# Second mixer of a two-layer encoder: activation tables fetched ahead, attention weights loaded beside the latent projection's, GpSimd multiplying its own taps in two of four channel tiles

## The chip, the cores and the metric

The kernel runs on one core of one Trainium2 chip. The metric is device time in microseconds (us) for one execution of the whole program. The kernel before takes 1110.24 us in the median of three runs (1110.16 to 1111.68).

## The reference

Two sequences of 256 tokens with 1024 features go through two layers. Each layer is a mixer and a feed-forward block, each followed by a residual sum and a layer norm. Only the second layer's mixer (`odd_mixer`) is touched:

```
h = x @ w_in                                   # 1024 -> 256 + 128 + 32 + 512 + 512
c_q, c_kv, k_r, glu_a, glu_g = split(h)
c = latent_attention(c_q, c_kv, k_r, ...)      # rmsnorm, q and k,v projections, rope, 8 heads, softmax
d = glu_a * sigmoid(glu_g)
d = silu(layernorm(dwconv(d, conv_w, conv_b))) # 31 taps along the tokens, 512 channels
return concat([c, d]) @ w_out
```

The other blocks are a first mixer (neighbourhood attention and spatial gating) and two convolutional feed-forward blocks of 2816 features (`ffn`).

## The kernel before

Both sequences are held together as 512 columns, features on the 128 partitions. Every product is done in three passes on a high and a low part (`hi`, `lo`) of weights and activations. A weight tile is fetched by SyncE's queue, rounded to `hi` by ScalarE (line 107) and reduced to `lo` by VectorE (line 109).

`odd_mixer` is written in the order glu(0), cproj, chain, glu(1), glu(2), kvproj, qproj, attend(0), glu(3), attend(1) to attend(3), flush, the first half of the output projection, the convolution's taps, `conv_ln`, the rest of the output projection. A scheduler with a model of the engines (`schedule_with_timeline_sim`) then sorts each engine's queue; each engine runs its queue strictly in order, and waits on semaphores for the others.

- `glu(i)` makes one of four tiles of 128 channels of the convolution's input (`dpad`): two products on TensorE, a sigmoid on ScalarE, a product on VectorE. It starts VectorE's accumulator `cacc` (tap 0 and the bias, in PSUM) and the second accumulator `acc` (`acc2` in the code).
- The 31 taps of a tile: VectorE does taps 0 to 20 on `cacc` (line 691). For taps 22 to 30 ScalarE multiplies (line 695, `pr`, a ring of two buffers) and GpSimd adds to `acc` (line 696); tap 21 starts `acc`. VectorE joins both (line 697).
- `cproj` and `chain` make the latent parts: after RMS norms and transposes, ScalarE writes the high and VectorE the low part of `cT` (lines 604, 605). `kvproj` and `qproj` read `cT` and write keys, values and queries.
- `attention` does a pair of heads and one sequence at a time. One unit (a head, a sequence) is: scores `s` on TensorE, row maximum `nmx` on VectorE (line 482), exponential on ScalarE (line 485), reciprocal `ri` on VectorE (line 488), scaling `er` on ScalarE (line 491), transposes `pt` on TensorE, a copy `PTr` on ScalarE (line 500). Two units are followed by one product `pv`. There are 16 units.
- `conv_ln` is the layer norm over the 512 channels: transposes `ct` to token tiles (four, t = 0 to 3), statistics on VectorE, the inverse root on GpSimd (line 162), the normalised `cnm` on VectorE, transposes `cb` back, Silu on ScalarE, and the split into `mixT[4..7]`. The last `ct` also releases GpSimd's residual products of tiles t = 2, 3 (`affine`).
- `OutProj`: its first group (attention's part) is summed by `op` (half 0) and `dn` (half 1) matmuls, its second group (the convolution's part) on top of them. The norm that follows ends in transposes `lnT`, and the next block starts with `up` matmuls.

Of the kernel before, what the change touches and what calls it, by code (L numbers as in the profile page):

```python
# [1 line left out]

# [6 lines left out]
F32 = mybir.dt.float32  # L9
# [3 lines left out]
ALU = mybir.AluOpType  # L13
# [37 lines left out]
def tile_encoder(ctx: ExitStack, tc: tile.TileContext, I, O):  # L51
# [46 lines left out]
    def after_mm(ins, m):  # L98
        tc.add_manual_dep(ins.ins, m.ins.name,
                          mybir.DependencyInfo(mybir.DependencyClass.Sync, mybir.DependencyReason.DATA),  # L100
                          reason="paced")

    def wload(src, n, keep=False):
        raw = rawp.tile([P, 1024], F32, tag="raw", name=nm("raw"))
# [24 lines left out]
    def pc(name, i):  # L129
        o, _ = PCOL[name]  # L130
        return par[:, o + i:o + i + 1]
# [152 lines left out]
    class OutProj:  # L284
# [12 lines left out]
        def step(self, k, t, half, w):  # L297
            gemm_tok([self.ps[half][t]], self.mixT[k], t, w[k][0], w[k][1], [slice(0, 512)],
                     k == self.g[0][0], k == self.g[1][-1])

        def first(self, half, ts=range(NT)):
            if self.ps[half] is None:
                self.ps[half] = [None] * NT if half == 0 else dn_banks()
                self.w1 = self.load(half, self.g[0])
            for t in ts:
                if half == 0:
                    self.ps[0][t] = bank(pA, "op0")
            for k in self.g[0]:
                for t in ts:
                    self.step(k, t, half, self.w1)  # L310
# [10 lines left out]
    def dn_banks():  # L321
        return [bank(pB if t < 2 else pC, "dn1") for t in range(NT)]
# [144 lines left out]
        return sink.xT  # L467

    pend = []

    def attention(p, score, V, mix, post, er, PTr, on_act=False):
        for s in range(2):
            PT = [PTr.get(), PTr.get()]
            pss = [bank(pB, "s").rearrange("p (a k) -> p a k", a=2) for _ in range(2)]
            for qt in range(2):
                for h in range(2):
                    score(pss[h][:, qt, :], h, slice(s * S + qt * P, s * S + qt * P + P), slice(s * S, s * S + S))
            for h in range(2):
                e = er.get()
                sc = post(pss[h], h, e)  # L480
                nmx = small(2, "nmx")
                nc.vector.tensor_reduce(out=nmx, in_=sc, axis=AX.X, op=ALU.max, negate=True)
                rs = small(2, "rs")
                for qt in range(2):
                    nc.scalar.activation(out=e[:, qt, :], in_=sc[:, qt, :], func=AF.Exp,
                                         bias=nmx[:, qt:qt + 1], accum_out=rs[:, qt:qt + 1])
                ri = small(2, "ri")
                nc.vector.reciprocal(out=ri, in_=rs)
                for qt in range(2):
                    if on_act:  # L490
                        nc.scalar.activation(out=e[:, qt, :], in_=e[:, qt, :], func=AF.Copy, scale=ri[:, qt:qt + 1])
                    else:
                        nc.vector.tensor_scalar(out=e[:, qt, :], in0=e[:, qt, :], scalar1=ri[:, qt:qt + 1],
                                                scalar2=None, op0=ALU.mult)
                pt = bank(pC, "pt")
                for kc in range(2):
                    for qt in range(2):
                        nc.tensor.transpose(pt[:, (2 * kc + qt) * P:(2 * kc + qt + 1) * P],  # L498
                                            e[:, qt, kc * P:(kc + 1) * P], ident)
                nc.scalar.copy(out=PT[h], in_=pt.rearrange("p (k q) -> p k q", k=2))  # L500

            def pv_stage(s=s, PT=PT):
                pv = bank(pC, "pv")
                for kc in range(2):
                    for h in range(2):
                        mm(pv[h * 64:(h + 1) * 64, :S], V[s][:, kc, (2 * p + h) * 64:(2 * p + h + 1) * 64],
                           PT[h][:, kc, :], kc == 0, kc == 1)
                split(mix, pv[:, :S], slice(s * S, s * S + S))
            flush_pv()
            pend.append(pv_stage)  # L510
# [10 lines left out]
    def odd_mixer(xT):  # L521
# [3 lines left out]
        def glu(i, by_seq=False):  # L525
            pss = []
            for hi, lo in kept.pop(i, None) or glu_load(i):
                pss.append((bank(pA, "glu"), hi, lo))
            for seqs in ((0,), (1,)) if by_seq else ((0, 1),):
                for ps, hi, lo in pss:  # L530
                    gemm_feat(ps, hi, lo, xT, seqs)
            sg = tmp([P, 512], s="sig")
            nc.scalar.activation(out=sg, in_=pss[1][0], func=AF.Sigmoid)
            d = dpad[i]
            nc.vector.tensor_tensor(out=d[:, :, 15:15 + S], in0=pss[0][0].rearrange("p (s t) -> p s t", s=2),
                                    in1=sg.rearrange("p (s t) -> p s t", s=2), op=ALU.mult)
            accps[i] = bank(pA, "cacc")
            a, a2 = accps[i].rearrange("p (s t) -> p s t", s=2), acc2[i // 2][:, i % 2]
            nc.vector.tensor_scalar(out=a, in0=d[:, :, 0:S], scalar1=pc("cw", i * 32),
                                    scalar2=pc("cw", i * 32 + 31), op0=ALU.mult, op1=ALU.add)  # L540
            nc.scalar.activation(out=a2, in_=d[:, :, 31 - NPOOL:31 - NPOOL + S], func=AF.Copy,  # L541
                                 scale=pc("cw", i * 32 + 31 - NPOOL))
# [14 lines left out]
        def cproj():  # L557
            psc = dn_banks()
            wc = [wload(I["wc"][:, 2 * k2:2 * k2 + 2, :].rearrange("p k n -> p (k n)"), 832) for k2 in range(4)]
            for s in range(2):  # L560
                for k in range(KC):
                    o = (k % 2) * 416
                    for t in (2 * s, 2 * s + 1):
                        gemm_tok([psc[t]], xT[k], t, *wc[k // 2], [slice(o, o + 416)], k == 0, k == KC - 1)
            G["psc"] = psc

        def chain():
# [27 lines left out]
            for i in (2, 0, 1, 3):  # L595
                w = P if i < 3 else 32
                for t in range(NT):
                    nc.tensor.transpose(ct_ps[i][0:w, t * P:(t + 1) * P],
                                        craw[t // 2][:, t % 2, i * P:i * P + w], ident)
                if i == 3:  # L600
                    nc.scalar.copy(out=krT[64:96, :], in_=ct_ps[3][0:32, :])
                else:
                    g = pc("qg", i) if i < 2 else pc("kvg", 0)
                    nc.scalar.activation(out=cT[i][:, 0, :], in_=ct_ps[i], func=AF.Copy, scale=g)
                    nc.vector.scalar_tensor_tensor(out=cT[i][:, 1, :], in0=ct_ps[i], scalar=g,
                                                   in1=cT[i][:, 0, :].bitcast(F32), op0=ALU.mult, op1=ALU.subtract)

        def qproj():
            cT = G["cT"]
            ropeT = act([P, 2, S], s="ropeT")  # L610
            after_mm(nc.gpsimd.dma_start(out=ropeT, in_=I["ropeT"]), G["start"])
            wq = [wload(I["wuq"][:, k, :], 1024) for k in range(2)]
            qT = G["qT"] = [act([P, 2, T], s="qT") for _ in range(4)]

            def qfeat(pool, c):
# [24 lines left out]

        def kvproj():
            cT, krT = G["cT"], G["krT"]
            wkv = wload(I["wukv"], 1024)
            V = G["V"] = [act([P, 2, 512], s="V1") for _ in range(2)]
            for t in range(NT):
                ps = bank(pB, "v1")
# [23 lines left out]
                      G["V"], mixT[p], lambda ps, h, e: ps, er, PTr, True)  # L670

        mixT = [None] * 8
        glu(0, True)
        cproj()
        chain()
# [1 line left out]
        glu(2)  # L677
        kvproj()
        qproj()
        attend(0)  # L680
        glu(3)
        for p in range(1, 4):
            attend(p)
        sink = G["sink"]
        flush_pv()
        op = OutProj("wout1", mixT, [0, 1, 2, 3], [4, 5, 6, 7])
        op.first(0, (0, 1))
        for i in range(4):
            a, a2 = accps[i].rearrange("p (s t) -> p s t", s=2), acc2[i // 2][:, i % 2]
            for j in range(1, 31 - NPOOL):  # L690
                nc.vector.scalar_tensor_tensor(out=a, in0=dpad[i][:, :, j:j + S], scalar=pc("cw", i * 32 + j), in1=a,  # L691
                                               op0=ALU.mult, op1=ALU.add)
            for j in range(32 - NPOOL, 31):
                pr = pr_ring.get()
                nc.scalar.activation(out=pr, in_=dpad[i][:, :, j:j + S], func=AF.Copy, scale=pc("cw", i * 32 + j))  # L695
                nc.gpsimd.tensor_tensor(out=a2, in0=a2, in1=pr, op=ALU.add)  # L696
            nc.vector.tensor_tensor(out=a2, in0=a, in1=a2, op=ALU.add)

        def conv_ln():
# [3 lines left out]
            for t in range(NT):  # L703
# [8 lines left out]
                n = tmp([P, 512], s="cnm")  # L712
                normalize(n, ps, mu, rstd)
                ns.append(n)
            for c in range(4):
                ps = bank(pA, "cb")
                for t in range(NT):
# [173 lines left out]
```

## Time and profile before

| what | us |
|---|---|
| median of three runs | 1110.24 |
| the profiled execution, whole | 1111.65 |
| its span | 1109.9 |
| TensorE busy in it | 1086.7 (98%) |
| VectorE, ScalarE, GpSimd busy in it | 663.3, 490.9, 224.0 |
| granted TensorE clock, mean | 0.986 |
| second mixer, from the first convolution input to the first `up` | about 574 to 738 |

The profile is of one execution. TensorE is busy nearly throughout, so the table of stages matters more than the totals: what can be won or lost is the time in which TensorE idles, or runs at a lower granted clock, in the second mixer.

### The profile page before, as it was taken

Reading aid. Unit: us, or ns where it says so; the run is one execution under the profiler, and the core shown is the slowest. Engines: PE = TensorE matmul, PEld = TensorE weight load, DVE = VectorE, ACT = ScalarE, POOL = GpSimd, SP = SyncE. Lnnn points to the kernel's source line nnn. Section 1 sums busy time; section 2 is a strip of 40 time slices with the busy share of each in tenths; the row PEclk is TensorE's granted clock in tenths of the full one; section 3 lists DMA queues with packets and bytes.
Section 4 is the critical chain, followed back from the end, with each engine's and each line's share of the span. In section 5 each row is a group of like instructions: output and inputs, shape, how many; then the busy total and the mean of one; then the engine's idle time right before and its main releaser. Section 6 shows DMA issues by size and latency. Waiting matters only on the chain. (4 is left out here: it accounts for less than half of the span.)

```text
span 1109.9 us, 13646 instructions
## 1 busy us (share of the span) xinstructions
PE 1086.7 (98%) x5210; PEld 902.8 (81%) x5210; DVE 663.3 (60%) x982; ACT 490.9 (44%) x789; POOL 224.0 (20%) x222
## 2 busy tenths in 40 slices
PE   9999999999999999999998979999999999999996
PEld 7888778988888888888897847789888888888885
DVE  5388956766565566422469897367656556552227
ACT  5435644544444444321365699446444444431110
POOL 0581002200000000006454757031000000000173
PEclk9999999999999999999999969999999999999998
DMA  7833222533333323654232221144333333222501
GB/s 263 247 107 95 72 101 96 171 95 97 96 101 103 98 95 114 197 184 138 76 117 76 60 93 67 57 135 132 96 97 101 103 98 96 95 95 95 211 36 76
DMA packets 36194, 124.34 MB, mean 112 GB/s; under 512 B 4353, under 2 KB 5121, under 8 KB 36129
## 3 DMA queue, kind: packets, MB, share of 16 engines
q1 hardware_dynamic: 28224, 99.00, 29.0%
q0 software_dynamic: 6480, 22.66, 5.9%
q10 hardware_dynamic: 1424, 1.80, 0.6%
q8 instruction: 41, 0.67, 0.3%
q14 instruction: 25, 0.20, 0.1%
HBM read 114.01 MB, written 8.39 MB: 110 GB/s over the span
## 5 line engine op out<-in xcount | busy, mean ns | idle before, releaser
L96 PE MATMUL up<-xT,whi 128*128 128x512 f32 (+1 forms) x1536 | 440.0, 371 | 0.0
L109 DVE TENSOR_TENSOR wlo<-raw,whi 128x1024 fp32r<-128x1024 f32 (+1 forms) x174 | 234.8, 1351 | 287.8 <-ACT whi L107 286.1
L96 PEld LDWEIGHTS up<-xT,whi 128*128 128x128 f32 x1536 | 279.9, 188 | 49.7
L107 ACT CAST whi<-raw 128x1024 fp32r<-128x1024 f32 (+1 forms) x174 | 182.3, 1050 | 246.3 <-PE dn L96 131.1
L96 PE MATMUL up<-xT,wlo 128*128 128x512 f32 (+1 forms) x768 | 283.8, 372 | 0.0
L96 PE MATMUL dn<-whi,gT 128*128 128x512 f32 x704 | 217.5, 389 | 0.0
L96 PEld LDWEIGHTS up<-xT,wlo 128*128 128x128 f32 x768 | 144.2, 188 | 25.1
L96 PEld LDWEIGHTS dn<-whi,gT 128*128 128x128 f32 x704 | 132.0, 188 | 27.2
L96 PE MATMUL dn<-wlo,gT 128*128 128x512 f32 x352 | 136.9, 389 | 0.0
L182 POOL DMA_DIRECT2D xres<-xscr x12 | 6.4, 540 | 574.7 <-PE dn L96 574.7
L96 PEld LDWEIGHTS dn<-wlo,gT 128*128 128x128 f32 x352 | 66.1, 188 | 13.7
L113 ACT CAST gT<-cv 128x512 fp32r<-128x512 f32 x44 | 27.3, 620 | 111.8 <-DVE cv L752 111.8
L741 ACT ACTIVATE cv<-up,par 128x512 f32<-128x512 f32 x88 | 68.2, 775 | 0.0
L744 DVE SCALAR_TENSOR_TENSOR cv<-up,par,cv 128x510 f32<-128x510 f32 x88 | 65.8, 748 | 2.7
L742 DVE SCALAR_TENSOR_TENSOR cv<-up,par,cv 128x510 f32<-128x510 f32 x88 | 65.4, 743 | 0.0
L751 ACT ACTIVATE cv<-cv 128x512 f32<-128x512 f32 x44 | 27.8, 632 | 83.3 <-DVE cv L744 83.3
L691 DVE SCALAR_TENSOR_TENSOR cacc<-dpad,par,cacc 128x512 f32<-128x512 f32 x80 | 59.0, 751 | 1.3
L696 POOL TENSOR_TENSOR acc<-acc,pr 128x512 f32<-128x512 f32 x36 | 49.9, 1386 | 37.3 <-ACT pr L695 35.2
L114 DVE TENSOR_TENSOR gT<-cv,gT 128x512 fp32r<-128x512 f32 x44 | 30.4, 692 | 27.5 <-ACT gT L113 27.5
L96 PE MATMUL op<-whi,mixT 128*128 128x512 f32 x128 | 44.0, 401 | 0.0
L96 PE MATMUL dn<-whi,mixT 128*128 128x512 f32 x128 | 43.0, 394 | 0.0
L96 PE MATMUL glu<-xT,khi 128*128 128x512 f32 (+1 forms) x160 | 42.2, 348 | 0.0
(192 smaller groups left out, 1348.0 us busy)
## 6 DMA issues: line engine op xcount, KB each, us to landing
raw<-in_wup SPq DMA_DIRECT2D x88, 512.0 KB, 3.7
raw<-in_wdn SPq DMA_DIRECT2D x44, 512.0 KB, 3.5
raw<-in_wout SPq DMA_DIRECT2D x16, 512.0 KB, 3.7
xscr<-xres POOLq DMA_DIRECT2D x12, 512.0 KB, 4.3
xres<-xscr POOLq DMA_DIRECT2D x12, 512.0 KB, 4.9
raw<-in_wqk SPq DMA_DIRECT2D x8, 512.0 KB, 5.8
raw<-in_wglu SPq DMA_DIRECT2D x8, 512.0 KB, 4.1
raw<-in_wug SPq DMA_DIRECT2D x7, 512.0 KB, 3.5
```

What stands on the lines that cost most here:

```text
L96: last_mm[0] = nc.tensor.matmul(out=out, lhsT=lhsT, rhs=rhs, start=first, stop=last)
L107: nc.scalar.copy(out=hi[:, :n], in_=raw[:, :n])
L109: nc.vector.tensor_tensor(out=lo[:, :n], in0=raw[:, :n], in1=hi[:, :n].bitcast(F32), op=ALU.subtract)
L113: nc.scalar.copy(out=dst[:, 0, sl], in_=src)
L114: nc.vector.tensor_tensor(out=dst[:, 1, sl], in0=src, in1=dst[:, 0, sl].bitcast(F32), op=ALU.subtract)
L182: after_mm(nc.gpsimd.dma_start(out=x, in_=src[t]), after)
L691: nc.vector.scalar_tensor_tensor(out=a, in0=dpad[i][:, :, j:j + S], scalar=pc("cw", i * 32 + j), in1=a, op0=ALU.mult, op1=ALU.add)
L696: nc.gpsimd.tensor_tensor(out=a2, in0=a2, in1=pr, op=ALU.add)
L741: nc.scalar.activation(out=c, in_=pv, func=AF.Identity, scale=pc(fw, ch * 4 + 1), bias=pc(fw, ch * 4 + 3))
L742: nc.vector.scalar_tensor_tensor(out=c[:, :, 1:S], in0=pv[:, :, 0:S - 1], scalar=pc(fw, ch * 4), in1=c[:, :, 1:S], op0=ALU.mult, op1=ALU.add)
L744: nc.vector.scalar_tensor_tensor(out=c[:, :, 0:S - 1], in0=pv[:, :, 1:S], scalar=pc(fw, ch * 4 + 2), in1=c[:, :, 0:S - 1], op0=ALU.mult, o ...
L751: nc.scalar.activation(out=cg, in_=cg, func=AF.Silu)
```

## The change

Five edits, all in the second mixer:

1. A one-element activation fetches each table (`preload`): Sigmoid before glu(0), Exp right behind the sigmoid of glu(3), Silu behind the last reciprocal of the softmax.
2. The weights of `kvproj` and `qproj` are requested inside `cproj`, and the first output weights by `op.open(0)` before the attention.
3. glu(3) is written before attend(0).
4. VectorE's taps 18 to 20 of channel tile 0 may only be issued after the low part of `cT` (`issue_after`).
5. In channel tiles 2 and 3 GpSimd, not ScalarE, multiplies the nine taps that it adds.

```diff
+    def preload(func, src):
+        nc.scalar.activation(out=small(1, "tab"), in_=src, func=func)
...
+        def open(self, half):
+            self.ps[half] = [None] * NT if half == 0 else dn_banks()
+            self.w1 = self.load(half, self.g[0])
...
             nc.scalar.activation(out=sg, in_=pss[1][0], func=AF.Sigmoid)
+            if i == 3:
+                preload(AF.Exp, sg[:, 0:1])
...
             wc = [wload(...) for k2 in range(4)]
+            G["wkv"] = wload(I["wukv"], 1024)
+            G["wq"] = [wload(I["wuq"][:, k, :], 1024) for k in range(2)]
...
-                    nc.vector.scalar_tensor_tensor(out=cT[i][:, 1, :], ...
+                    G["cT_lo"] = nc.vector.scalar_tensor_tensor(out=cT[i][:, 1, :], ...
...
         mixT = [None] * 8
+        preload(AF.Sigmoid, xT[0][:, 0, S:S + 1].bitcast(F32))
         glu(0, True)
...
-        attend(0)
         glu(3)
-        for p in range(1, 4):
+        op = OutProj("wout1", mixT, [0, 1, 2, 3], [4, 5, 6, 7])
+        op.open(0)
+        for p in range(4):
             attend(p)
...
             for j in range(1, 31 - NPOOL):
-                nc.vector.scalar_tensor_tensor(out=a, in0=dpad[i][:, :, j:j + S], ...
+                with tc.issue_after(G["cT_lo"].ins) if i == 0 and j >= 18 else nullcontext():
+                    nc.vector.scalar_tensor_tensor(out=a, in0=dpad[i][:, :, j:j + S], ...
             for j in range(32 - NPOOL, 31):
                 pr = pr_ring.get()
-                nc.scalar.activation(out=pr, in_=dpad[i][:, :, j:j + S], func=AF.Copy, scale=pc("cw", i * 32 + j))
+                if i < 2:
+                    nc.scalar.activation(out=pr, in_=dpad[i][:, :, j:j + S], func=AF.Copy,
+                                         scale=pc("cw", i * 32 + j))
+                else:
+                    nc.gpsimd.tensor_scalar(out=pr, in0=dpad[i][:, :, j:j + S], scalar1=pc("cw", i * 32 + j),
+                                            scalar2=None, op0=ALU.mult)
                 nc.gpsimd.tensor_tensor(out=a2, in0=a2, in1=pr, op=ALU.add)
...
+            preload(AF.Silu, last_ri[0])
             for c in range(4):
                 ps = bank(pA, "cb")
```

The change moves instructions in four queues; SyncE's is the same, row for row. First VectorE's queue at the end of `chain`, before (`cacc` numbers tell the channel tiles apart: 4533 is tile 0, 4802 tile 1):

```order
L587 TENSOR_TENSOR craw_4693<-ra_4710,rb_4711 128x32
L691 SCALAR_TENSOR_TENSOR cacc_4533<-dpad_4412,par,cacc_4533 128x512 x7
L697 TENSOR_TENSOR acc_704_4424<-cacc_4533,acc_704_4424 128x512
L605 SCALAR_TENSOR_TENSOR cT_4662<-dn_755_4724,par,cT_4662 128x512
L605 SCALAR_TENSOR_TENSOR cT_4660<-dn_753_4722,par,cT_4660 128x512
L605 SCALAR_TENSOR_TENSOR cT_4661<-dn_754_4723,par,cT_4661 128x512
L535 TENSOR_TENSOR dpad_4415<-glu_4749,sig_4799 128x2x256
```

And the same place now (4535 is tile 0, 4822 tile 1):

```order
L599 TENSOR_TENSOR craw_4713<-ra_4730,rb_4731 128x32
L706 SCALAR_TENSOR_TENSOR cacc_4535<-dpad_4412,par,cacc_4535 128x512 x4
L617 SCALAR_TENSOR_TENSOR cT_4682<-dn_765_4744,par,cT_4682 128x512
L617 SCALAR_TENSOR_TENSOR cT_4680<-dn_763_4742,par,cT_4680 128x512
L617 SCALAR_TENSOR_TENSOR cT_4681<-dn_764_4743,par,cT_4681 128x512
L706 SCALAR_TENSOR_TENSOR cacc_4535<-dpad_4412,par,cacc_4535 128x512
L545 TENSOR_TENSOR dpad_4415<-glu_4769,sig_4819 128x2x256
```

Three taps and the joining add moved from ahead of `cT` to behind it.

Second, TensorE's queue at the convolution's layer norm. Before, the transposes `ct` of t = 2 and t = 3 (5676, 5690) stand inside the attention:

```order
L96 MATMUL s_5357<-kT_4892,qT_4938 128x256 x2
L707 MATMUL ct_5676<-ident,acc_704_4424 128x128 x2
L707 MATMUL ct_5676<-ident,acc_705_4425 128x128 x2
L96 MATMUL s_5358<-kT_4892,qT_4938 128x256 x2
L707 MATMUL ct_5690<-ident,acc_704_4424 128x128 x2
L707 MATMUL ct_5690<-ident,acc_705_4425 128x128 x2
L498 MATMUL pt_5328<-ident,er_5022 128x128 x4
L498 MATMUL pt_5343<-ident,er_5022 128x128 x4
L96 MATMUL s_5400<-kT_4892,qT_4938 128x256 x2
```

Now all but three of the `ct` transposes (5652, 5666, 5680, 5694 are t = 0 to 3) stand behind the last matmul of the first output group, and the first `cb` follows them directly:

```order
L96 MATMUL dn_954_5749<-wlo_5760,mixT_5372 128x512
L96 MATMUL dn_954_5749<-whi_5758,mixT_5372 128x512
L727 MATMUL ct_5652<-ident,acc_705_4425 128x128
L727 MATMUL ct_5666<-ident,acc_704_4424 128x128 x2
L727 MATMUL ct_5666<-ident,acc_705_4425 128x128 x2
L727 MATMUL ct_5680<-ident,acc_704_4424 128x128 x2
L727 MATMUL ct_5680<-ident,acc_705_4425 128x128 x2
L727 MATMUL ct_5694<-ident,acc_704_4424 128x128 x2
L727 MATMUL ct_5694<-ident,acc_705_4425 128x128 x2
L739 MATMUL cb_5714<-ident,cnm_5664 128x128
L739 MATMUL cb_5714<-ident,cnm_5678 128x128
L739 MATMUL cb_5714<-ident,cnm_5692 128x128
```

No other TensorE work stands any more between the `ct` of the four token tiles and the first `cb`.

Third, GpSimd's queue in channel tile 3. Before, the 18 adds of tiles 2 and 3 stand in one piece, ahead of the residual's fetches:

```order
L611 DMA ropeT_4921<-in_ropeT 128x512
L696 TENSOR_TENSOR acc_705_4425<-acc_705_4425,pr_4428 128x512 x18
L182 DMA xres_5167<-xscr 128x1024
L182 DMA xres_5169<-xscr 128x1024
L182 DMA xres_5171<-xscr 128x1024
L182 DMA xres_5173<-xscr 128x1024
L173 DMA rowg_5175<-in_rows 128x1024
```

Now, from the third tap of tile 3 on (dpad_4421):

```order
L714 TENSOR_SCALAR pr_4428<-dpad_4421,par 128x512
L185 DMA xres_5183<-xscr 128x1024
L176 DMA rowg_5191<-in_rows 128x1024
L176 DMA rowb_5192<-in_rows 128x1024
L714 TENSOR_SCALAR pr_4428<-dpad_4421,par 128x512
L716 TENSOR_TENSOR acc_705_4425<-acc_705_4425,pr_4428 128x512
L193 TENSOR_TENSOR xres_5183<-xres_5183,rowg_5191 128x1024
L193 TENSOR_TENSOR xres_5185<-xres_5185,rowg_5191 128x1024
L716 TENSOR_TENSOR acc_705_4425<-acc_705_4425,pr_4428 128x512
L714 TENSOR_SCALAR pr_4428<-dpad_4421,par 128x512
L196 TENSOR_TENSOR xres_5183<-xres_5183,rowb_5192 128x1024
L196 TENSOR_TENSOR xres_5185<-xres_5185,rowb_5192 128x1024
```

The six fetches and four residual products now stand between the tap multiplies and adds of tile 3. (Three more `xres` fetches stand beside the first one; they are left out here.)

## Rows read from the trace of the kernel before

**Rows 1.** Page, costliest groups: out<-in xcount | busy, mean ns | idle before, releaser
```profile
L109 DVE TENSOR_TENSOR wlo<-raw,whi 128x1024 fp32r<-128x1024 f32 (+1 forms) x174 | 234.8, 1351 | 287.8 <-ACT whi L107 286.1
L107 ACT CAST whi<-raw 128x1024 fp32r<-128x1024 f32 (+1 forms) x174 | 182.3, 1050 | 246.3 <-PE dn L96 131.1
```

**Rows 2.** Stages: window and its length; busy us (count) per engine; PEclk; DMA; GB/s
```profile
602.16:605.20 3.04, 3.04 (x7) 2.46 (x8) 2.97 (x5) 0.03 (x1) 0.00 (x0) 0.50 0.01 3
643.90:667.85 23.95, 17.14 (x49) 10.13 (x49) 21.87 (x37) 22.43 (x55) 14.04 (x15) 0.57 0.38 132
667.85:709.70 41.85, 41.13 (x243) 31.37 (x242) 21.98 (x53) 32.71 (x90) 20.85 (x12) 1.00 0.08 26
709.70:738.46 28.76, 28.76 (x136) 23.99 (x135) 15.05 (x33) 10.62 (x17) 3.73 (x6) 1.00 0.40 125
```

**Rows 3.** Timeline of TensorE: start, length, instruction, [idle before <-releaser]
```profile
602.16 1.22 PE L96 MATMUL k<-cT,whi 128*128 128x512 f32 x2 [3.58 <-DVE cT L605]
...
647.10 2.07 PE L96 MATMUL s<-kT,qT 96*128 96x256 f32 x4 [3.00 <-ACT er L485]
```

**Rows 4.** Timeline of VectorE, from the end of chain to the last reciprocal
```profile
595.15 5.51 DVE L691 SCALAR_TENSOR_TENSOR cacc<-dpad,par,cacc 128x512 f32<-128x512 f32 x7
...
601.36 2.06 DVE L605 SCALAR_TENSOR_TENSOR cT<-dn,par,cT 128x512 fp32r<-128x512 f32 x3
...
620.20 3.38 DVE L691 SCALAR_TENSOR_TENSOR cacc<-dpad,par,cacc 128x512 f32<-128x512 f32 x5
...
647.08 0.17 DVE L488 RECIPROCAL ri<-rs 128x2 f32<-128x2 f32 x1 [0.82 <-ACT er L485]
...
669.43 0.16 DVE L488 RECIPROCAL ri<-rs 128x2 f32<-128x2 f32 x1
...
674.33 1.30 DVE L157 BATCH_NORM_STATS2 st<-ct 128x6 f32<-128x512 f32 x2 [0.77 <-PE ct L707]
...
690.76 1.52 DVE L166 TENSOR_SCALAR cnm<-ct,mv,rstd 128x512 f32<-128x512 f32 x2
...
692.20 0.15 DVE L488 RECIPROCAL ri<-rs 128x2 f32<-128x2 f32 x1
```

**Rows 5.** Timeline of ScalarE: a table load, and Silu with its cast
```profile
572.20 1.28 ACT L533 ACT_TABLE_LOAD   x1 [7.94 <-PE glu L96]
573.49 0.60 ACT L533 ACTIVATE sig<-glu 128x512 f32<-128x512 f32 x1
...
706.05 1.42 ACT L719 ACTIVATE cb<-cb,par 128x512 f32<-128x512 f32 x2 [4.89 <-PE cb L718]
707.39 1.08 ACT L113 CAST mixT<-cb 128x512 fp32r<-128x512 f32 x2
```

**Rows 6.** Timeline of GpSimd: adds, fetches, residual products, roots
```profile
607.07 12.28 POOL L696 TENSOR_TENSOR acc<-acc,pr 128x512 f32<-128x512 f32 x9 [11.50 <-ACT pr L695]
...
660.89 2.12 POOL L182 DMA_DIRECT2D xres<-xscr  x4
...
671.09 4.68 POOL L190 TENSOR_TENSOR xres<-xres,rowg 128x1024 f32<-128x1024 f32 x2 [7.05 <-DMA rowg<-in_rows]
...
684.41 4.67 POOL L190 TENSOR_TENSOR xres<-xres,rowg 128x1024 f32<-128x1024 f32 x2 [2.00 <-PE ct L707]
689.04 1.07 POOL L162 TENSOR_TENSOR rstd<-rstd,epsc 128x1 f32<-128x1 f32 x2
...
740.38 0.75 POOL L245 TENSOR_TENSOR xT<-xv,xT 128x256 fp32r<-128x256 f32 x1 [0.56 <-DVE xT L243]
```

**Rows 7.** Chain that ended last, in order of time: start, us, what
```profile
686.07 1.01 PE pv L96 x8
...
735.90 2.72 PE dn L96 x12
...
738.62 7.67 PE up L96 x64
746.30 0.87 PE lnT L233 x8
```

More of the change, by code (lines that the diff above doesn't have):

```diff
@@ L1 @@
-from contextlib import ExitStack
+from contextlib import ExitStack, nullcontext
 import concourse.bass as bass
@@ L299, in step @@
                      k == self.g[0][0], k == self.g[1][-1])
+        def open(self, half):
+            self.ps[half] = [None] * NT if half == 0 else dn_banks()
+            self.w1 = self.load(half, self.g[0])
         def first(self, half, ts=range(NT)):
             if self.ps[half] is None:
-                self.ps[half] = [None] * NT if half == 0 else dn_banks()
-                self.w1 = self.load(half, self.g[0])
+                self.open(half)
             for t in ts:
@@ L469, in tile_encoder @@
     pend = []
+    last_ri = [None]
     def attention(p, score, V, mix, post, er, PTr, on_act=False):
@@ L488, in attention @@
                 nc.vector.reciprocal(out=ri, in_=rs)
+                last_ri[0] = ri[:, 0:1]
                 for qt in range(2):
@@ L604, in chain @@
                     nc.scalar.activation(out=cT[i][:, 0, :], in_=ct_ps[i], func=AF.Copy, scale=g)
-                    nc.vector.scalar_tensor_tensor(out=cT[i][:, 1, :], in0=ct_ps[i], scalar=g,
-                                                   in1=cT[i][:, 0, :].bitcast(F32), op0=ALU.mult, op1=ALU.subtract)
+                    G["cT_lo"] = nc.vector.scalar_tensor_tensor(out=cT[i][:, 1, :], in0=ct_ps[i], scalar=g,
+                                                                in1=cT[i][:, 0, :].bitcast(F32), op0=ALU.mult,
+                                                                op1=ALU.subtract)
         def qproj():
@@ L611, in qproj @@
             after_mm(nc.gpsimd.dma_start(out=ropeT, in_=I["ropeT"]), G["start"])
-            wq = [wload(I["wuq"][:, k, :], 1024) for k in range(2)]
+            wq = G["wq"]
             qT = G["qT"] = [act([P, 2, T], s="qT") for _ in range(4)]
@@ L642, in kvproj @@
             cT, krT = G["cT"], G["krT"]
-            wkv = wload(I["wukv"], 1024)
+            wkv = G["wkv"]
             V = G["V"] = [act([P, 2, 512], s="V1") for _ in range(2)]
@@ L685, in odd_mixer @@
         flush_pv()
-        op = OutProj("wout1", mixT, [0, 1, 2, 3], [4, 5, 6, 7])
         op.first(0, (0, 1))
@@ L690, in odd_mixer @@
             for j in range(1, 31 - NPOOL):
-                nc.vector.scalar_tensor_tensor(out=a, in0=dpad[i][:, :, j:j + S], scalar=pc("cw", i * 32 + j), in1=a,
-                                               op0=ALU.mult, op1=ALU.add)
+                with tc.issue_after(G["cT_lo"].ins) if i == 0 and j >= 18 else nullcontext():
+                    nc.vector.scalar_tensor_tensor(out=a, in0=dpad[i][:, :, j:j + S], scalar=pc("cw", i * 32 + j),
+                                                   in1=a, op0=ALU.mult, op1=ALU.add)
             for j in range(32 - NPOOL, 31):
                 pr = pr_ring.get()
-                nc.scalar.activation(out=pr, in_=dpad[i][:, :, j:j + S], func=AF.Copy, scale=pc("cw", i * 32 + j))
+                if i < 2:
[4 more added lines that the diff above has]
+                                            scalar2=None, op0=ALU.mult)
                 nc.gpsimd.tensor_tensor(out=a2, in0=a2, in1=pr, op=ALU.add)
```

## The prediction

> **What bounds the kernel now.** I read the costliest groups first, then the stages, then the timelines of the engines inside the one stage that has holes, and last the chain of waits. TensorE is the bound: before and after the second mixer's attention it has no gap, so an edit counts only where TensorE idles or runs at the lower granted clock. The stages show three such places [rows 2, 3]. TensorE waits 3.58 us for `cT`, and then runs 3.04 us at a granted clock of 0.50, half of 2.4 GHz. From 643.90 to 667.85, at the start of the softmax, it is busy 17.14 of 23.95 us at a clock of 0.57. After that, up to the first `up` matmul at 738.46, it is busy 41.13 of 41.85 and 28.76 of 28.76 us at a clock of 1.00. So the whole layer norm of the convolution, which falls in 674 to 707, costs TensorE nothing today: other matmuls lie over it. That cover is what the new order touches.
>
> **The change, part by part.** All times are on the axis of the profiled execution, whose own time is 1111.65 us (span 1109.9), 1.4 above the median of the runs.
>
> *Loads.* SyncE's queue is the same in both kernels, row for row; the requests written earlier were already issued there. I cost this edit at nothing, and that part of the change does not do what its words say.
>
> *The Sigmoid table.* The load, 1.28 us, now runs while ScalarE is idle for 7.94 us ahead of it [rows 5]. It is off TensorE's path (VectorE's queue goes on being full behind it): 0, at most 1.3 gained.
>
> *`cT`.* Seven passes in 5.51 us stand ahead of it; three of them and the joining add leave, 3 x 0.79 + 0.69 = 3.1 us [rows 4]. TensorE's wait of 3.58 shrinks to 0.5, and with it goes the half clock behind it, worth 1.5 [rows 2, 3]. TensorE comes 4.6 us earlier to the end of the projections, 639.3 for 643.9.
>
> *The first softmax unit.* What is late next is VectorE. From the end of `cT` (601.36 + 2.06 = 603.4) to the first reciprocal (647.08) its queue took 43.7 us [rows 4]. Counted in the new order, this stretch has three taps and a join more from tile 0 (3.1), two `wlo` more (2 x 1.35, rows 1) and three taps of tiles 2 and 3 fewer (3 x 0.72, between 3.38/5 where two accumulators alternate and 0.79 where one is repeated). That is +3.6; 0.8 of waiting at the reciprocal goes. So 46.5 us from 600.3: the first reciprocal comes at 646.8, as before. TensorE's gain of 4.6 is then idle time ahead of the softmax, since glu(3) no longer lies between its units. Bounds: 641, if VectorE's other waits in the stretch vanish too, and 649.
>
> *The units.* The fifteen intervals between reciprocals took 45.1 us: the last nine 22.8 (2.53 each, from 669.43), the first six 22.3 [rows 4]. In the first six ScalarE also did eight tap multiplies and two casts, some 8 x 0.6 + 2 x 1.05 = 6.9 us [rows 1, 5], which leave. VectorE still has two to three taps a unit there, and TensorE starts at half clock, so I take 3.0 each, 18.0 in all. The last reciprocal then comes at 646.8 + 18.0 + 22.8 = 687.6, 4.6 us earlier. Bounds: 2.53 each, 684.8, and no gain, 692.
>
> *To the transposes.* Behind it: scaling 0.9 and its pipeline, to 689.1; the Silu load, now ahead of the last two copies, 1.3; its one-element activation 0.2; two copies 1.1; one `pv` 1.0 [rows 5, 7]; then 36 matmuls of the first output group, at 2.72 / 12 = 0.227 each, 8.2 [rows 7]. TensorE reaches the `ct` transposes at 701. The other condition is GpSimd. Its multiply is not in the trace; with one input of 512 elements it lies between the 256-column operation that also reads 512, 0.75, and the 512-column add, 1.36 [rows 6]. I take the middle, 1.05. Its first fetch of the residual now waits for the first `pv`, at about 658 (four units and the product), with 16 of the taps' instructions of tile 3 behind it. Then: six issues at 0.53, 661; multiply and add 2.4, hidden under the landing, 7.05 after the last issue, 668; products 4.7; add and multiply 2.4; products 4.7; four multiplies and five adds 11.0; 691; VectorE's join 0.7. That is 9 us before 701, so the multiplies are free, by 0.75 as by 1.36.
>
> The Trainium skill (GPSIMD Engine Reference, Engine selection) sends elementwise work to VectorE and calls GpSimd about half as fast with two inputs, but near line rate with one. Its Performance versus the Vector engine section has 0.77 us for 512 elements in a tight loop; by that estimate the sum stays as it is, since the 9 us stand. No run so far shows the operation.
>
> *The layer norm.* In the new queue nothing lies between the four `ct` and the first `cb`, so its chain is paid in full. From the first `ct`: five transposes 0.55, but VectorE first does a `wlo` whose cast waits for the last matmul of the group, so the statistics start after about 1.6; two statistics 1.3; a second `wlo` 1.35; four small operations 0.6; a root 0.54; a normalisation 0.76: 6.2 [rows 1, 4, 6]. Only then are banks free for t = 2 and 3: eight transposes at half clock, 1.8: 8.0. GpSimd was released by the last of them and first does two residual products, 4.67, then two roots, 1.07 (the same order as at 684.41): 13.7. A normalisation 0.76, the last `cb` 0.2, Silu 0.71 and its cast 0.54 [rows 5]: 15.9, and some fourteen hand-overs between engines at 0.1: 17.3 us to the first matmul of the second group.
>
> *The rest.* 120 matmuls 27.2, eight `cb` 0.9, sixteen `lnT` 1.7, and 1.5 for a clock that has fallen in the wait: 31.3. The first `up` comes at 701 + 17.3 + 31.3 = 749.6 for 738.46: +11.1. Before, 64 `up` matmuls, 7.67 us, stood ahead of the last two token tiles' `lnT` [rows 7]; now 39, 4.7 us, while ScalarE squares both tiles behind eight other activations. I add 2.4 (0 to 4). Sum: +13.5, 1125.1 on the profile's count, 1123.7 on the median's; rounded down, 1123.
>
> The row of the table load has the sigmoid start 1.29 us after the load [rows 5]. The Trainium skill (ScalarE: Activation LUTs, What ACT_TABLE_LOAD costs) gives 2.66 us for a switch, with a drain behind the load. By it the Silu load ahead of the last copies would cost 1.4 more and the sum would be 1125; the row shows no such drain, and I keep 1.28.
>
> **Rivals.** *A: the front really frees.* VectorE's waits vanish, the first reciprocal comes at 641, all intervals are 2.53, the last is at 679, `ct` at 692.5. The clock does not fall, the `wlo` are done in time: 17.3 - 2.4 - 0.9 = 14.0, then 29.8 without a clock loss, no gap at `lnT`: `up` at 736.3, a gain of 2.2, 1108; two more microseconds and it is 1106. It decides once `ct` starts before about 694. For it: ScalarE loses 18 of 36 tap multiplies and TensorE's wait for `cT` is real. Against it: VectorE's count, and ScalarE's own 2.53 a unit. *B: the gain at the front and the exposed norm cancel*, `ct` at about 695, within 2 us of 1110. *C: GpSimd sets the end.* With a multiply of 2.7, twice the two-input add, tile 2 ends at 656 and tile 3 at 708; the norm starts at 709, with its `wlo` done, 5 us later than forecast: 1128 to 1130. It decides from about 2.0 a multiply. Against it: both rows of bounds. *D: more clock loss*, the softmax at half clock up to its middle and the second group starting at half clock for as long as after 643.90: 5 to 8 more, up to 1131.
>
> **How the numbers follow.** Forecast 0.60, own range 1117 to 1128; A 0.13, B 0.10, C 0.07, D 0.10. A measurement of this kernel can tell about 0.2%, 2.2 us, from no change. A gives 0.10 faster and 0.03 same; B 0.06 same, 0.02 faster, 0.02 slower; the others are slower: faster 0.12, same 0.09, slower 0.79. The range that holds 8 in 10 reaches down into A and B and up to C and part of D: 1109 to 1130.
>
> **What would show it.** Right: `k` starts near 599 with no idle over 1 us; the first reciprocal is between 644 and 649; TensorE idles some 5 us inside the `ct` transposes and some 6 ahead of `cb`, with a lower granted clock in both; GpSimd's last tap add ends before the first `ct` of t = 1. Wrong: `ct` starts before 694; or the statistics find TensorE busy; or GpSimd's multiply is above 2 us.

## The result, and the profile after

The changed kernel takes 1123.26 us in the median of four runs (1122.19 to 1124.35), the kernel before 1110.85 in the four beside them: a ratio of 1.0111, 95% interval 1.0094 to 1.0129. It is slower by 12.4 us; forecast were 1123 and "slower". The profiled execution's span is 1122.2 us for 1109.9.

The stages after, as in [rows 2]: window and its length; busy us (count) of TensorE, its weight loads, VectorE, ScalarE, GpSimd; granted clock; DMA.

```profile
599.38:644.01 44.63, 41.42 (x179) 34.06 (x180) 43.20 (x63) 27.18 (x46) 37.23 (x26) 0.97 0.22 55
644.01:682.68 38.67, 37.10 (x189) 25.63 (x189) 29.82 (x62) 35.50 (x110) 34.05 (x27) 0.90 0.26 94
682.68:694.90 12.22, 12.15 (x66) 9.43 (x65) 1.70 (x4) 4.71 (x9) 6.35 (x5) 1.00 0.00 0
694.90:712.93 18.03, 6.96 (x30) 5.39 (x29) 9.68 (x20) 4.16 (x6) 11.06 (x8) 0.63 0.21 60
712.93:722.00 9.07, 9.07 (x37) 7.28 (x37) 2.07 (x3) 2.68 (x4) 0.35 (x1) 0.80 0.00 0
```

The fourth row is new: TensorE is busy for 6.96 of 18.03 us, at a clock of 0.63, and the next 9 us still run at 0.80. Before, TensorE had no such stretch behind 667.85. The list of what TensorE waited for from 540 us on (us, times, longest), before:

```profile
PE s L96 <- ACT er L485: 4.1, 2, 3.0
PE k L96 <- DVE cT L605: 3.6, 1, 3.6
PE pt L498 <- ACT er L491: 2.7, 2, 1.6
PE pv L96 <- ACT PTr L500: 0.7, 1, 0.7
PE dn L96 <- ACT xv L242: 0.5, 1, 0.5
```

and after:

```profile
PE cb L739 <- DVE cnm L169: 6.2, 1, 6.2
PE ct L727 <- DVE cnm L169: 4.2, 1, 4.2
PE s L96 <- DVE wlo L112: 3.2, 1, 3.2
PE up L96 <- DVE xT L246: 2.4, 1, 2.4
PE up L96 <- DVE xT L248: 1.6, 1, 1.6
PE s L96 <- ACT er L492: 1.1, 2, 0.8
PE op L96 <- ACT mixT L116: 0.6, 1, 0.6
PE dn L96 <- ACT xv L245: 0.5, 1, 0.5
PE pt L506 <- ACT PTr L508: 0.4, 1, 0.4
PE k L96 <- DVE cT L617: 0.3, 1, 0.3
```

The lists sum to 11.6 and 20.5 us. TensorE's busy time over the span rose from 1086.7 to 1090.1 with the same 5210 matmuls: that is the slower clock. 8.9 + 3.4 = 12.3, the whole difference of the spans. The waits for `cT` and inside the softmax went down by 6.1; two for the norm (10.4), one behind it (0.6) and two for `xT` (4.0) came, and their clock.

TensorE's timeline through the norm (the end of the last `dn` is at 696.0):

```profile
696.00 0.71 PE L727 MATMUL ct<-ident,acc 128*128 128x128 f32 x5
700.96 1.94 PE L727 MATMUL ct<-ident,acc 128*128 128x128 f32 x8 [4.25 <-DVE cnm L169]
...
709.11 1.96 PE L739 MATMUL cb<-ident,cnm 128*128 128x128 f32 x8 [6.22 <-DVE cnm L169]
...
711.68 0.80 PE L96 MATMUL op<-whi,mixT 128*128 128x512 f32 x1 [0.60 <-ACT mixT L116]
```

Nothing but the transposes runs for 15.7 us. VectorE's first and last reciprocal of the softmax, and the sum that ends the convolution (channel tile 3), against [rows 4]:

```profile
644.01 0.15 DVE L495 RECIPROCAL ri<-rs 128x2 f32<-128x2 f32 x1
...
682.68 0.17 DVE L495 RECIPROCAL ri<-rs 128x2 f32<-128x2 f32 x1 [0.50 <-ACT er L492]
...
689.23 0.69 DVE L717 TENSOR_TENSOR acc<-cacc,acc 128x512 f32<-128x512 f32 x1 [0.57 <-POOL acc L716]
```

Before, the softmax ended at 692.2, and that last sum came at 671.74, 20 us ahead of it. Now the softmax ends 9.5 us earlier and the sum comes 7 us behind it. GpSimd's timeline, the last multiply and add of that sum and then the residual product that stands ahead of the second pair of roots, against [rows 6]:

```profile
686.26 1.55 POOL L714 TENSOR_SCALAR pr<-dpad,par 128x512 f32<-128x512 f32 x1
...
687.90 1.30 POOL L716 TENSOR_TENSOR acc<-acc,pr 128x512 f32<-128x512 f32 x1
...
702.98 4.64 POOL L193 TENSOR_TENSOR xres<-xres,rowg 128x1024 f32<-128x1024 f32 x2 [2.48 <-PE ct L727]
707.57 1.07 POOL L165 TENSOR_TENSOR rstd<-rstd,epsc 128x1 f32<-128x1 f32 x2
```

All multiplies as one group, from 600 to 720 us (busy us, mean ns):

```profile
L714 POOL TENSOR_SCALAR pr<-dpad,par 128x512 f32<-128x512 f32 x18 | 28.2, 1575 | 0.1
```

### The profile page after: what moved, and what is told of

Same layout as the page of the kernel before. It is cut to its first block, busy times and chain, and to the rows that moved or that the text cites. A ratio compares the mean times of both kernels' runs of the same rounds, so it can differ in the third digit from the quotient of the medians.

```text
span 1122.2 us, 13639 instructions
## 1 busy us (share of the span) xinstructions
PE 1090.1 (97%) x5210; PEld 906.3 (81%) x5210; DVE 663.5 (59%) x982; ACT 480.6 (43%) x774; POOL 253.7 (23%) x240
## 4 chain that ended last, share of the span: by engine, by line
PE 91%; DVE 4%; ACT 2%; POOL 1%; issue 1%; DMA 1%; POOLq 0%; DVEq 0%; ACTq 0%
PE up L96 43%; PE dn L96 28%; PE qk L96 4%; PE op L96 4%; PE glu L96 3%; PE v L96 2%; PE u L96 2%; PE s L96 2%; PE pv L96 1%; PE pt L506 1%; DVE wlo L112 1%; DVE cacc L706 1%; PE lnT L236 1%; ACT er L499 0%; ACT er L492 0%
```

## The experiments

The theory: the loss is the norm of the convolution, which now stands bare in TensorE's queue, and it comes from edit 5 alone; the other edits together gain. The rivals: another edit costs; or GpSimd's multiplies cost by themselves, wherever they stand. "The planner" below is the scheduler that sorts the engines' queues: each edit is written in the program, and the planner's new order comes with it. Each time is a median, with its ratio to the kernel before that ran beside it (median 1111.0 to 1111.5).

### Runs 1 and 2: edit 5 undone, and then the old loss put back by order alone

Run 1 (the changed kernel, ScalarE multiplying every tap):

```diff
-                if i < 2:
...
-                else:
-                    nc.gpsimd.tensor_scalar(out=pr, in0=dpad[i][:, :, j:j + S], scalar1=pc("cw", i * 32 + j),
-                                            scalar2=None, op0=ALU.mult)
+                nc.scalar.activation(out=pr, in_=dpad[i][:, :, j:j + S], func=AF.Copy, scale=pc("cw", i * 32 + j))
```

> The changed kernel, but ScalarE multiplies the taps of all four channel tiles, as before. With that one edit undone the planner writes the ct and cb transposes between the softmax units again (TensorE's queue has ct 5, 4, 4 among the last units). Theory: what costs the 12.4 us is that TensorE stands over the layer norm with nothing else in its queue, 4.2 + 6.2 us of idle time plus the half clock behind each; with the transposes back among the units these two waits go. ScalarE takes back 18 multiplies of 0.6 us, 10.8 us, most of it inside the softmax, where it is the pace; so the gain of the front is largely spent: 1104 to 1111 us. Rival (the other edits are to blame: the table loads, the moved glu(3), the early weights): it stays above 1118 us.

Run 2 (run 1, with `conv_ln` written behind `op.first(1)` and the transposes ordered behind that call's last matmul, `behind`):

```diff
-                    tr = nc.tensor.transpose(ps[:, c * P:(c + 1) * P],
-                                             acc2[c // 2][:, c % 2, s, q * P:(q + 1) * P], ident)
+                    with tc.issue_after(behind.ins):
+                        tr = nc.tensor.transpose(ps[:, c * P:(c + 1) * P],
+                                                 acc2[c // 2][:, c % 2, s, q * P:(q + 1) * P], ident)
...
-        conv_ln()
         w1 = op.w1
         op.first(1)
+        conv_ln(last_mm[0])
```

> The kernel of the first run with one thing more: the ct transposes are ordered behind the first output group's dn matmuls on TensorE, so that nothing stands between them and the first cb, as in the changed kernel, while ScalarE still multiplies every tap. Theory (the order is what costs): 10 to 15 us slower than the first run, near 1118 to 1126, with waits of about 4 and 6 us for cnm. Rival (GpSimd's multiplies themselves are what costs, by ending the convolution late): within 3 us of the first run.

Measured: run 1 1104.75 us, 0.9945 (0.9930 to 0.9960); run 2 1126.58, 1.0140 (1.0123 to 1.0157). In run 1 the last sum comes at 668 and the norm runs under the softmax (VectorE's row, then TensorE's):

```profile
668.02 0.68 DVE L712 TENSOR_TENSOR acc<-cacc,acc 128x512 f32<-128x512 f32 x1
```

```profile
669.53 0.71 PE L722 MATMUL ct<-ident,acc 128*128 128x128 f32 x5
...
679.46 0.66 PE L722 MATMUL ct<-ident,acc 128*128 128x128 f32 x4 [0.76 <-DVE cnm L169]
...
692.00 0.76 PE L734 MATMUL cb<-ident,cnm 128*128 128x128 f32 x5
```

0.76 us is all that TensorE waits for the norm. In run 2 it waits for it as in the changed kernel:

```profile
PE cb L735 <- DVE cnm L169: 6.2, 1, 6.2
...
PE ct L723 <- DVE cnm L169: 3.9, 1, 3.9
```

The theory holds, and the order alone costs 21.8 us, more than the 10 to 15 expected: waits grew by 14.4, of which the expectation named the 10 for `cnm` and not the 4.0 for `xT`, and TensorE's busy time by 7.5 (1084.8 to 1092.3, the same 5210 matmuls) from the slower clock. ScalarE multiplies every tap here, and the last sum is there at 669, as in run 1: the place in TensorE's queue is enough for the loss, without a late sum.

### Run 4: edit 5 alone; run 8: edit 4 alone

Both are the kernel before with one edit: the `nc.gpsimd.tensor_scalar` branch, or the `issue_after(G["cT_lo"].ins)` of taps 18 to 20.

> The kernel before with this edit alone: GpSimd multiplies its own taps in channel tiles 2 and 3. Its TensorE queue has the same bare layer norm (ct 13, cb 8 with nothing between) as the changed kernel. Theory: the whole loss comes from this edit, and the rest of the change gives back 4 to 5 us (the earlier cT): 1124 to 1130 us. Rival (the loss comes from the sum of edits): under 1118 us.

> The kernel before with one edit: taps 18 to 20 of channel tile 0 stand behind cT on VectorE. Theory (the prediction's step): TensorE's wait of 3.58 us shrinks to about 0.4 and the half clock behind it goes, 4.6 us, but VectorE's queue sets the start of the softmax, so part of it comes back as a longer wait there: 1105 to 1109 us. Rival A (all of the gain is kept): 1104 to 1106 us. Rival B (all of it comes back): 1109.5 to 1112 us.

Measured: run 4 1130.07 us, 1.0171 (1.0156 to 1.0187), at the upper end of what was expected; run 8 1105.84, 0.9950 (0.9935 to 0.9965). So edit 5 costs 19.0 and edit 4 gains 5.6, which lies in the theory's range and in rival A's. The 4.6 that the step was expected to be worth are kept whole, so nothing of them came back at the softmax, and rival B is out. Edits 1 to 4 together gain 6.3 (run 1), and 19.0 - 6.3 = 12.7 is the measured 12.4 of all five. Between runs 1 and 8 (0.9945 and 0.9950, with intervals that overlap) edits 1 to 3 make no difference that can be measured.

### Runs 5, 6 and 12: where the multiplies stand, and their price

Run 5; run 6 has 3 in place of 2:

```diff
-                if i < 2:
+                if not (i == 2):
```

> The changed kernel with GpSimd multiplying its taps in channel tile 2 alone (nine multiplies instead of eighteen). The first four runs left this: the layer norm is a chain of some 18 us on VectorE and GpSimd, and it costs nothing only when it can start that far ahead of the softmax's end; the sum of channel tile 3 ended at 689.9 in the changed kernel and at 668.7 in the first run. Theory (when tile 3's sum ends decides): tile 2's multiplies are done early, in time in which GpSimd waited for ScalarE, so tile 3's sum ends near 672, the transposes stand among the softmax units, and the time is that of the first run or a little less: 1101 to 1106 us. Rival (each multiply on GpSimd costs, wherever it stands): half of the 18.3 us that lie between the changed kernel and the first run: about 1114 us.

> The same number of multiplies, nine, but in channel tile 3 alone. Theory (when tile 3's sum ends decides): they stand behind the residual's fetches and products, tile 3's sum ends near 685, and only the transposes of the first token tiles come ahead of other matmuls: 1115 to 1123 us. Rival (the number of multiplies decides): the same time as the run with tile 2, within 2 us.

Measured: 1104.51 us (0.9939, 0.9922 to 0.9955) with tile 2 and 1121.63 (1.0092, 1.0077 to 1.0107) with tile 3: nine multiplies of the same length are free in one place and cost 17 us in the other. The number of them is not what costs. The last sum of run 5, and of run 6 with TensorE's rows:

```profile
673.28 0.69 DVE L717 TENSOR_TENSOR acc<-cacc,acc 128x512 f32<-128x512 f32 x1
```

```profile
682.14 0.69 DVE L717 TENSOR_TENSOR acc<-cacc,acc 128x512 f32<-128x512 f32 x1
```

```profile
689.05 0.71 PE L727 MATMUL ct<-ident,acc 128*128 128x128 f32 x5
...
696.00 1.03 PE L727 MATMUL ct<-ident,acc 128*128 128x128 f32 x8
...
704.23 0.87 PE L739 MATMUL cb<-ident,cnm 128*128 128x128 f32 x3 [7.20 <-DVE cnm L169]
```

In run 6 the sum is there at 682.8, but the transposes stand behind other matmuls in TensorE's queue, and the remaining thirteen run only from 689 on. The planner had written them late.

Run 12 shortens each multiply of the changed kernel: it takes the first of the two sequences alone and leaves the products of the other out of the computation.

```diff
-                    nc.gpsimd.tensor_scalar(out=pr, in0=dpad[i][:, :, j:j + S], scalar1=pc("cw", i * 32 + j),
+                    nc.gpsimd.tensor_scalar(out=pr[:, 0:1, :], in0=dpad[i][:, 0:1, j:j + S], scalar1=pc("cw", i * 32 + j),
```

> The changed kernel with GpSimd's multiplies cut to one of the two sequences, 256 elements instead of 512 (the other half is left out of the computation), so that one takes about 0.8 us instead of 1.57, the price that the prediction's lower bound came near to. Theory: the price of the multiply decides after all, by the end of tile 3's sum: 18 x 0.75 us less puts it near 676, the planner writes ct and cb among the softmax's last units and the output's dn matmuls, and the time is 1102 to 1107 us, at least 16 us less than the changed kernel. Rival (at any price between 0.75 and 1.36 the norm is bare and the multiplies are free, as the prediction had it): 1118 us or more.

Measured: 1108.51 us, 0.9976 (0.9966 to 0.9985): 14.8 less than the changed kernel, above the theory's range by 1.5 and far from the rival's 1118. The multiply takes on average what the prediction had taken (GpSimd's group):

```profile
L714 POOL TENSOR_SCALAR pr<-dpad,par 128x256 f32<-128x256 f32 x18 | 18.8, 1055 | 0.1
```

The last sum then comes at 677.76. The plan changes with the shape, so this run does not part the chip's price from the planner's idea of it.

### Runs 3, 7 and 9: the norm's own length

Run 3 keeps all five edits and orders the 48 `dn` matmuls of the first group into the holes; run 7 moves the late residual products behind the roots instead; run 9 does both. The lines with `behind` and `self.step` are run 3's (`behind` has, for each k of `op.first(1)`, the transpose that it waits behind), the rest is run 7's.

```diff
+                    with tc.issue_after(self.behind[i].ins) if half == 1 and self.behind else nullcontext():
+                        self.step(k, t, half, self.w1)
...
-                if t == NT - 1:
-                    sink.res.affine([u for u in range(NT) if u not in EARLY], tr)
+            with tc.issue_after(last_root[0].ins):
+                sink.res.affine([u for u in range(NT) if u not in EARLY], tr)
...
+        op.behind = [G["tr1"], G["tr1"], G["tr3"], G["tr3"]]
```

> The changed kernel with GpSimd's multiplies kept, but the 48 dn matmuls of the first output group are ordered behind the transposes: 24 behind ct of the second token tile, 24 behind ct of the fourth. Theory (the order is what costs): the two holes of 4.2 and 6.2 us are filled with 5.5 us of matmuls each, and the clock doesn't fall; TensorE waits 1 to 2 us for the last tap's sum at about 690 instead: 1111 to 1115 us. Rival (GpSimd's multiplies cost): within 2 us of the changed kernel's 1123.

> The changed kernel with the two residual products of the late token tiles (4.67 us on GpSimd) ordered behind the second pair of roots instead of ahead of it. Theory: they are 4.64 of the 6.22 us for which TensorE waits ahead of cb, so that wait falls to about 1.6 us and the time to 1117 to 1120 us. Rival (the wait is VectorE's statistics and normalisation): wait and time stay, 1121 to 1124 us.

> The third run (the first output group's 48 dn matmuls in the holes of the layer norm, GpSimd multiplying in two tiles) gained nothing, although the transposes started 5.2 us earlier. Theory: the chain of the norm got as much longer, 20.0 us from the first ct to the first op matmul instead of 15.7, because the residual products on GpSimd stand ahead of the second pair of roots, and VectorE's two weight conversions run at 2.7 instead of 1.2 us beside them. Here the products are ordered behind the roots as well: the chain falls to about 15 us, the first op matmul comes near 706, and the time is 1115 to 1119 us, less than with the products moved alone (1119.5). Rival (TensorE's own order of matmuls makes the third run no faster): 1119 to 1123 us.

Measured: run 3 1123.00 us, 1.0111 (1.0095 to 1.0126), no gain; run 7 1119.49, 1.0073 (1.0058 to 1.0088); run 9 1114.06, 1.0031 (1.0019 to 1.0042), 0.9 below what was expected. Run 3's expectation failed, and its rival's number came, but not for the rival's reason. The first of its thirteen late `ct` is at 690.78, 5.2 earlier than in the changed kernel, and the `op` matmul behind the norm at 710.83, 0.9 earlier: the chain grew from 15.7 to 20.0 us. VectorE's and GpSimd's rows of run 3:

```profile
698.69 2.75 DVE L112 TENSOR_TENSOR wlo<-raw,whi 128x1024 fp32r<-128x1024 f32 x1
...
704.95 2.63 DVE L112 TENSOR_TENSOR wlo<-raw,whi 128x1024 fp32r<-128x1024 f32 x1
```

```profile
697.96 5.73 POOL L193 TENSOR_TENSOR xres<-xres,rowg 128x1024 f32<-128x1024 f32 x2 [4.07 <-PE ct L729]
703.64 0.55 POOL L165 TENSOR_TENSOR rstd<-rstd,epsc 128x1 f32<-128x1 f32 x1
704.16 2.34 POOL L196 TENSOR_TENSOR xres<-xres,rowb 128x1024 f32<-128x1024 f32 x1
706.46 1.53 POOL L165 TENSOR_TENSOR rstd<-rstd,epsc 128x1 f32<-128x1 f32 x1
```

Between the statistics and the last root lie a weight conversion of 2.75 us, two products of 5.73 together (4.64 in the changed kernel) and then, between the two roots, a third product; the last root takes 1.53 us beside the second conversion, where the one ahead of it takes 0.55. With the products behind the roots (run 9) the chain is 15.3 us from `ct` at 690.18 to `op` at 705.48, TensorE's waits for `cnm` vanish from its list, and 9 us come back. Run 9 is still 9.3 us behind run 1. Its last sum comes at 689.4 for 668.0, and TensorE waits 1.5 us for it; no run parts the rest.

### Runs 10 and 11: the fastest, and glu(3)

Run 10 is run 5 with the products behind the roots; run 11 is run 5 with glu(3) written behind `attend(0)` again.

> The candidate for the fastest: GpSimd multiplies in channel tile 2 alone, and the late residual products are ordered behind the second pair of roots. Theory: the layer norm is covered in the run with tile 2 already, so what shortens its chain gives little: the same as that run or up to 2 us less, 1102 to 1105 us. Rival (the end of the norm still holds TensorE up somewhere behind it): 1100 us or less.

> The run with GpSimd's multiplies in tile 2, with glu(3) written behind the first head pair's attention again, as before. Theory (when tile 3's sum ends decides): the taps of tile 3 can start later and end later, by 5 to 8 us, the transposes move towards the softmax's end, part of the norm is bare, and the time is 1106 to 1114 us, so that the moved glu(3) is worth several us here. Rival (the moved glu(3) is worth nothing by itself, since its matmuls only change places with the softmax's first wait): within 2 us of that run's 1104.5.

Measured: 1103.83 us (0.9929, 0.9915 to 0.9944), the lowest, and 1104.76 (0.9940, 0.9925 to 0.9955). Both beat both kernels; runs 1, 5, 10 and 11 can't be told apart. Run 11 went the rival's way: its last sum comes 6.6 us later than run 5's, at 679.89, and costs nothing, since the planner still writes the transposes among the softmax's last work: the first five of the late thirteen ahead of the last scores `s`, the other eight (686.24) ahead of the last two `pv`.

```profile
680.64 0.77 PE L728 MATMUL ct<-ident,acc 128*128 128x128 f32 x5
681.25 1.03 PE L96 MATMUL s<-kT,qT 96*128 96x256 f32 x4
```

In run 6 all thirteen come behind the softmax's last `pv`. So it is not the sum's end by itself that decides, but where the plan puts the transposes; run 11 (679.9) and run 6 (682.1) lie 2 us apart in the one and 17 us in the time.

## Why the prediction was right, and where not

The mechanism was right: TensorE paid for the norm, because nothing else stood in its queue there. Its terms, in order:

- *Loads and tables*: predicted 0, and runs 1 and 8 show no difference from them. The Silu load took the 1.28 us of its row, and the activation behind it started 1.29 after the load (683.81 to 685.10).
- *`cT`*: `k` starts at 599.4 with 0.33 of idle, predicted 599 and 0.5. By itself (run 8) it gains 5.6 for 4.6.
- *The first reciprocal*, predicted 646.8, came at 644.0. The step that failed is "0.8 of waiting at the reciprocal goes", which left VectorE's other waits as they were. VectorE's work between `cT` and that reciprocal rose by 3.2 (38.74 to 41.92), as counted (3.6), but its waits fell by 3.5 (4.92 to 1.44): the one for the rotary table (1.1) went whole, and those for the sigmoids fell from 2.3 to 0.9.
- *The units*: 38.7 us for the predicted 40.8; the first six took 2.6 each, not 3.0.
- *To the transposes*: 13.3 us for 13.4. So `ct` came at 696.0 for 701, all of it from the two points above.
- *GpSimd's multiply* was mis-sized: 1.575 us for 1.05, above the bound of 1.36. The sum ended at 689.9 for 691.7 all the same, because its fetches stood at 654.4 and not at 658 and the multiplies ran from 617 on. (Thirteen instructions of tile 3 stood behind the fetches, as its sum counts them, not the 16 of its words.) That the multiplies "are free, by 0.75 as by 1.36" held for the queue as written, where `ct` came 6 us behind the sum. It hid that the same multiplies had moved the transposes there: runs 1, 5 and 12 show other plans with them elsewhere, shorter or gone.
- *The norm*: 15.7 us for 17.3, waits of 4.25 and 6.22 for "some 5 and some 6". The hand-overs at 0.1 that lift its sum from 15.9 to 17.3 had no row behind them; two that can be read here take 0.06 (the cast that ends at 711.62, to `op`) and 0.08 (the last `ct`, to GpSimd's product). Run 7 confirms the product in front of the roots: without it the second wait is 2.4.
- *The rest*: 34.9 us from the first `op` to the first `up` for 31.3. Of the 3.6 too few, 2.4 are the wait for `xT`, counted behind the first `up` in the prediction. `up` starts 8.1 us later than before, predicted 11.1; behind it 4.2 more come for 2.4, since from 742 to 760 the clock is 0.81.

The sum is 12.3 for 13.5 on the spans: -4.9 at the front, -0.1, -1.6 in the norm, +3.6 and +1.8 behind it. So the nearness of 1123 owes something to errors of both signs. Rivals A and B had the price wrong: `ct` at 696.0 is 1 us from B's 695, for which it gave "within 2 us of 1110", and the kernel was 12.4 slower; they left out the waits for `xT` and the clock. C's 2.0 a multiply was not reached. D came in part, inside the forecast's range: a clock of 0.76 from 644.01 to 660 and 1.00 behind it in the softmax, and 0.80 in the first 9 us of the second group.

Run 2 sets the price of the place in the queue: with the early sum of run 1 and the late place it takes 1126.58, 3.3 more than the changed kernel, so the late place alone is enough for the whole loss of edit 5. What stays open is what the late sum costs by itself, that is, how much of the loss would stay if the transposes stood as early as the sums allow: such an order was tried only in run 9's form. Why the planner chose the late place is not shown either.

## What to carry to other kernels

In these runs a chain of small operations between two engines was free when its first link stood far enough ahead of the busy engine's last other work (runs 1, 5 and 11) and cost its waits and the clock when it stood behind it (runs 2 and 4); an edit that shortens that work and lengthens the way to the chain's start loses twice. Read from the queue order what lies between the chain's links on the bound engine before any duration. Filling the hole is worth only what the chain doesn't give back in length: look at which other instructions the two engines have in it.

## What the runs showed of the hardware

*One input was not cheaper than two on GpSimd.* In the changed kernel a multiply of 512 columns by a number per partition takes 1.575 us on average, the sum of two tensors of that size 1.30 (the timeline above) and 1.364 on average, other work beside both. In run 12, 256 columns take 0.91 to 0.94 in most places and 1.055 on average. By the Trainium skill (GPSIMD Engine Reference, Performance versus the Vector engine) the prediction had 0.77 for 512 columns as an estimate; no run agrees.

*A conversion on VectorE and a product on GpSimd take turns.* In run 9 the same conversion runs alone and beside the products:

```profile
698.10 1.21 DVE L112 TENSOR_TENSOR wlo<-raw,whi 128x1024 fp32r<-128x1024 f32 x1
...
703.63 2.84 DVE L112 TENSOR_TENSOR wlo<-raw,whi 128x1024 fp32r<-128x1024 f32 x1 [1.85 <-ACT whi L110]
```

```profile
700.70 4.69 POOL L195 TENSOR_TENSOR xres<-xres,rowg 128x1024 f32<-128x1024 f32 x2
705.35 5.75 POOL L198 TENSOR_TENSOR xres<-xres,rowb 128x1024 f32<-128x1024 f32 x2
```

The second conversion starts inside a product that ends at 705.39 and itself ends at 706.47, 1.08 later; the products behind it take 1.06 more than the 4.69 of the first pair. So, by these lengths, the one stood still until the other's instruction was over, in turn. The Trainium skill (SBUF — State Buffer, Terms) describes such a lock between these two engines, held for a whole instruction, and the trace agrees. Not every pair does this: in the changed kernel two multiplies from 646.71 on take 3.10 us together beside VectorE's taps (three in 2.06), whose accumulator lies in PSUM.
